# Two written instruction orders, VectorE's and ScalarE's, changed in a fused conformer and SSD block

## The chip, the cores and the metric

The kernel runs on one core of a Trainium2 chip. The metric is the device time of one execution in microseconds, and the figure compared is the median of several runs. One more execution was recorded by the hardware profiler; all durations below are from it. The engines are called as in the profile: PE is TensorE, which multiplies matrices (PEld is its loading of weights), DVE is VectorE, ACT is ScalarE, POOL is GpSimd, and SP is SyncE, which only issues loads and stores here.

## The reference: what is computed

One block of a network on 512 tokens of width 1024, in float32. Cut to what matters:

```python
h = rms_norm(x, mix_pre_g)
proj = h @ w_in                       # u_glu, z, x/B/C, dt and two gates
v = val * sigmoid(gt)                 # of u_glu + glu_b
v = silu(layer_norm(causal_depthwise_conv(v, 31 taps)))
conv_out = v @ pw_w + pw_b
x, B, C = silu(causal_depthwise_conv(xbc, 4 taps))
y = ssd_chunked(x, dt, a, B, C, d_skip) * silu(z)
y = y * rsqrt(mean(y * y over each of 8 groups) + eps) * norm_g
ssm_out = y @ out_w
mixed = (g_conv * conv_out + g_ssm * ssm_out) @ w_out
x = x + rms_norm(mixed)
x = x + rms_norm((silu(g) * u) @ w_down)   # g, u of rms_norm(x) @ w_gate_up
```

`ssd_chunked` is the state-space scan: inside a chunk of tokens it forms C B^T, weighs it with a lower triangle of decays exp(a_cs[l] - a_cs[s]) and multiplies it with x dt; between chunks it carries a state.

## The kernel before

**Products.** Every factor is held as a high part, rounded to the format fp32r, and a low part, the remainder; `mm3` (L423) makes each product of three matmuls, high by high (L425), low by high (L427 or L431, by the side) and high by low. Activations are split once. Weights are split as they arrive: SP loads 512 KB into one of five `raw` buffers (L382), ScalarE casts the high part `whi` (L390), and VectorE subtracts it from raw to make `wlo` (L397). For every second block of the scan ScalarE writes the negated high part (L394) and a GpSimd DMA adds the raw weights to it (L395). `whi` and `wlo` have five buffers each, in rotation; in the w_out stage some blocks use a second pair, `chi` and `clo`. A `raw` buffer is loaded again once both of its readers are done.

**Stages.** (1) Norm and the gated projection, to about 103 us. (2) The scan, to about 510 us, in 8 groups g. For a group, `proj_x` and `proj_bc` project x (two tiles), B and C into PSUM; `conv4` runs the 4-tap convolution on each, a scaled copy by ScalarE (L887, the step x_g_e.0), three taps by VectorE (L889) and a SiLU by ScalarE (L893). `make_L` (from L670) broadcasts the running sums into the tile L by a GpSimd DMA, masks it by a GpSimd `affine_select` (L675), and ScalarE takes 16 exponentials of it (L681). `s1` (L943) transposes x on TensorE into `pxT`, in two halves, each in its own bank, from which VectorE makes `xdt` (L957), part of `y` (L958) and `xdec` (L962); it also forms C B^T (`pcb`) and multiplies L by it (L973). `s2` (L976) forms the chunk states (`pSa`, `pSb`, from `xdec`), the carried states `prev` (L985, L988) and the diagonal part `yd`. `s3` (L999) adds the part from the carried state (`yo`, L1013), multiplies by silu(z), and normalises: squares on ScalarE (`jk`, L1032), the mean and the power on GpSimd (`power`, `pm` at L436, `rs` at L437), and a scaled copy on ScalarE (`y`, L1035). `s4` (L1039) transposes y (`pyT`) and splits it into a high part by ScalarE (L1050) and a low part by VectorE (L1051); both are called `yhl`. `proj_zz` (L922) projects z for two groups at once, four tiles `pz`, each emptied by ScalarE in two SiLUs, `zb` (L938) and `z` (L939). `ssm_out` multiplies finished pairs of groups by the output weights (`pso`). Between these stand the taps of the 31-tap convolution, on VectorE (`tap`, L698; a0 to a7 are the eight tiles of channels), with the first tap of each on ScalarE (L695), and sums over channels (`vsum`, L1155). (3) The gates and the rest of `ssm_out`, to about 600 us. (4) The pointwise product of the convolution branch, in forms that save products (from L1258), about 600 to 641 us; it ends in `mixed` (L1269), which adds the two branches in `pd` (L1270) and splits them into `m0h`, `m1h` (ScalarE, L1273) and `m0l`, `m1l` (VectorE, L1274), for the two halves of the tokens. (5) w_out (`tm_wo`, about 631 to 686 us), whose result is normalised and added to the input rows `xr` (L1468), loaded through ScalarE's queue, as is the gain `gpost0` (L1385). (6) The feed-forward part, to the end.

**Banks.** PSUM has eight banks. The scan's short-lived tiles (`pxT`, `pyT`, `pSa`, `pYa`) take three of them in turn, the projections (`px`, `pB`, `pC`, `pz`, `pso`) another three in turn, and `yd`, `pBT` and `pcb` the other two. A tile that TensorE wants to write waits until the tile that stood in its bank has been read: the second half of a pxT waits for `yhl` of the pyT that is three places before it, the fourth `pz` for `zb` and `z` of the first.

**Orders.** Nothing decides at run time. Five lists of names, one per engine, give the order in which each executes: `ORDER_ACT` (from L94), `ORDER_DVE` (from L164), `ORDER_PE` (from L250), `ORDER_POOL` (L260) and `ORDER_SP` (L273). `in_written_order` (L338) counts each engine's instructions by the tile they write, calls them name.0, name.1 and so on, and ties each to the one before it in the list, without a semaphore; an engine takes its instructions one after the other, and one that waits holds up all behind it. A DMA that ScalarE issues stands in its list like any other step. In ScalarE's list y1.0 is the scaled copy of L1035, in VectorE's list y1.4 is one of the products of `s3`; x0_1.1 is in ScalarE's list the SiLU of the second x tile of group 0, in VectorE's its second tap.

Of the kernel before, what the change touches and what calls it, by code (L numbers as in the profile page):

```python
# [61 lines left out]
for _n, _c in PRM:  # L62
# [36 lines left out]
    "h_t13.3 h_t42.0 h_t42.2 h_t42.1 h_t13.1 sg2.0 h_t42.3 sg3.0 z0.2 whi_11S.0 whi_11s.0 z0.0 whi_11C.0 z0.3 a0.0 "  # L99
    "z0.1 whi_13S.0 v4.0 v5.0 v4.1 whi_15A.0 a1.0 sg4.0 scratch.0 whi_13C.0 whi_17A.0 wlo_17A.0 v6.0 v5.1 sg5.0 "  # L100
    "whi_15S.0 whi_13s.0 sg4.2 whi_15C.0 whi_17S.0 sg4.1 sg5.2 whi_19.0 sg5.1 v7.0 v6.1 wlo_19.0 sg6.0 sg6.1 "
    "whi_17C.0 whi_20.0 v7.1 sg7.0 sg6.2 whi_21.0 wlo_21.0 whi_22.0 cd.0 scratch.2 eacs.0 sg7.2 whi_23.0 scratch.3 "
    "wlo_23.0 scr.3 sg7.1 whi_24.0 scr.0 x0_0.0 scr.1 dec.0 whi_25.0 scr.2 wlo_25.0 x0_1.0 x0_0.1 whi_26.0 B0.0 "
    "x0_1.1 L0.0 L0.4 L0.2 L0.1 L0.5 L0.3 C0.0 L0.7 L0.8 L0.6 L0.9 B0.1 C0.1 L0.10 x1_0.0 L0.14 x1_1.0 L0.11 L0.12 "
    "L0.13 L0.15 whi_27.0 x1_0.1 BT0.0 wlo_27.0 whi_28.0 whi_29.0 L1.0 B1.0 prev0.0 wlo_29.0 whi_30.0 L1.1 x1_1.1 "
    "B1.1 L1.2 C1.0 whi_31.0 L1.3 wlo_31.0 L1.4 L1.5 L1.6 L1.7 L1.8 L1.9 z1.0 C1.1 jk.0 L1.10 jk.1 whi_32.0 z1.1 jk.2 "
    "jk.3 L1.15 L1.11 L1.13 L1.14 x2_0.0 y0.1 L1.12 y0.2 y0.0 L2.0 y0.3 whi_33.0 whi_34.0 wlo_33.0 whi_35.0 BT1.0 "
    "x2_1.0 wlo_35.0 x2_0.1 L2.2 B2.0 L2.1 yhl0.0 whi_36.0 L2.4 prev1.0 B2.1 x2_1.1 L2.3 L2.5 C2.0 whi_37.0 L2.6 "
    "wlo_37.0 yhl0.1 C2.1 L2.7 L2.8 L2.9 L2.10 jk.4 L2.11 jk.5 L2.12 jk.6 L2.13 jk.7 L2.14 L2.15 L3.0 L3.1 L3.2 L3.3 "
    "y1.0 y1.1 zb2_0.0 z2.0 zb2_0.1 z2.1 y1.2 y1.3 L3.4 zb2_1.0 whi_38.0 z2.2 whi_39.0 whi_40.0 wlo_39.0 zb2_1.1 z2.3 "  # L110
# [6 lines left out]
    "zb4_0.0 z4.0 zb4_0.1 z4.1 y3.0 y3.1 y3.2 y3.3 zb4_1.0 z4.2 L5.14 whi_54.0 whi_55.0 whi_56.0 wlo_55.0 zb4_1.1 "  # L117
    "whi_57.0 x5_0.0 whi_58.0 a4.0 z4.3 a5.0 yhl2.2 yhl2.3 x5_1.0 L5.15 BT4.0 whi_59.0 wlo_57.0 B5.0 x5_0.1 whi_60.0 "
    "wlo_59.0 whi_61.0 x5_1.1 prev4.0 wlo_61.0 B5.1 whi_62.0 C5.0 whi_63.0 wlo_63.0 C5.1 L6.0 whi_64.0 L6.1 L6.2 L6.3 "
# [63 lines left out]
    "prev1.1 a1.29 vsum.0 C2.0 C2.1 C2.2 yhl0.1 yo1.0 yo1.1 y1.4 y1.5 wlo_38.0 wlo_40.0 x3_0.0 x3_0.1 wlo_42.0 x3_0.2 "  # L183
# [1789 lines left out]
```

## Time and profile before

| | us |
|---|---|
| median of 3 runs | 1014.97 (1014.56 to 1015.54) |
| the profiled execution | 1014.45 |
| its span | 1012.7 |
| PE busy | 1001.7 (99%) |
| PEld busy | 881.7 (87%) |
| DVE busy | 875.5 (86%) |
| ACT busy | 672.7 (66%) |
| POOL busy | 124.0 (12%) |

The span goes from the first to the last recorded instruction; 1.75 us of the profiled execution lie around it. Shares are of the span. TensorE was granted 0.999 of its full clock. A row of a timeline gives the start, the duration, the engine, the line, the operation with its output and inputs, and in brackets the idle time of the engine before it and what released it. In the list of waits a row gives who waited for whom, the sum, the number of times and the longest. In the chain of waits a row gives a start, a duration and what stood on the chain. In the table by stage a row gives the stretch and its length, and then for PE, PEld, DVE, ACT and POOL the busy time and the number of instructions, the granted clock, the share of the DMA engines and GB/s. Durations in a timeline overlap a little, because the next instruction starts before the last has drained: the distance from start to start is what one costs. A row of a helper such as `mm3` carries the helper's line, so the tile's name tells the stage.

### The profile page before, as it was taken

How to read it: one execution, taken by the hardware profiler on the slowest of the kernel's cores; microseconds unless marked ns; L12 is line 12 of the kernel's file. 1: busy time of each engine (PE TensorE's matmuls, PEld its weight loads, DVE VectorE, ACT ScalarE, POOL GpSimd, SP SyncE). 2: the span in 40 equal slices, each digit the busy share in tenths (PEclk: the TensorE clock that was granted, in tenths of full speed). 3: DMA queues.
4: the chain of work that ended last, by engine and by line, in shares of the span. 5: the costliest groups of instructions: out<-in, count | busy, mean ns of one | idle time of the engine just before them, and what ended most of it. 6: DMA issues, size and time to landing. Idle time of an engine off the chain costs nothing.

```text
span 1012.7 us, 16327 instructions
## 1 busy us (share of the span) xinstructions
PE 1001.7 (99%) x6296; PEld 881.7 (87%) x6296; DVE 875.5 (86%) x1285; ACT 672.7 (66%) x1104; POOL 124.0 (12%) x145
## 2 busy tenths in 40 slices
PE   9999999999999999999999999999999999999997
PEld 7899889878888888888888889889999999998886
DVE  7898999828997999899996688779999897899974
ACT  8577798898667756873442585587666566668552
POOL 0210211110123122110110020011000000001001
PEclk9999999999999999999999999999999999999999
DMA  8756945637641874365452256636555455469622
GB/s 299 215 133 154 256 121 148 186 95 177 167 146 23 212 188 121 97 157 141 104 134 94 83 116 210 216 109 165 184 146 167 147 146 146 135 178 290 210 84 83
DMA packets 44557, 156.62 MB, mean 155 GB/s; under 512 B 5184, under 2 KB 6208, under 8 KB 43456
## 3 DMA queue, kind: packets, MB, share of 16 engines
q1 hardware_dynamic: 30672, 105.44, 30.9%
q0 software_dynamic: 11888, 44.57, 22.5%
q10 hardware_dynamic: 1920, 5.57, 1.6%
q8 instruction: 49, 0.80, 0.3%
q14 instruction: 28, 0.23, 0.1%
HBM read 151.31 MB, written 4.26 MB: 154 GB/s over the span
## 4 chain that ended last, share of the span: by engine, by line
PE 80%; ACT 9%; DVE 7%; POOL 1%; issue 1%; DMA 1%; POOLq 0%; DVEq 0%; ACTq 0%; SPq 0%
PE xy L431 4%; PE xy L425 4%; PE xy L427 4%; PE pso L425 3%; PE pso L431 3%; PE pso L427 3%; PE yv L431 2%; PE yv L427 2%; PE yv L425 2%; DVE a L698 2%; PE px L425 2%; PE px L427 2%; PE px L431 2%; ACT whi L390 2%; PE pgs L431 1%; PE pgc L425 1%
## 5 line engine op out<-in xcount | busy, mean ns | idle before, releaser
L698 DVE SCALAR_TENSOR_TENSOR a<-v,prm_t,a 128x507 f32<-128x507 f32 (+19 forms) x240 | 171.9, 760 | 0.5
L390 ACT CAST whi<-raw 128x1024 fp32r<-128x1024 f32 x91 | 94.4, 1046 | 87.6 <-PE pso L427 42.5
L397 DVE TENSOR_TENSOR wlo<-raw,whi 128x1024 fp32r<-128x1024 f32 x54 | 65.7, 1220 | 34.3 <-ACT whi L390 34.3
L395 POOL DMA_DIRECT2D wlo<-in_w x37 | 32.9, 890 | 283.3 <-ACT wlo L394 97.8
L425 PE MATMUL pz<-whi,hhi 128*128 128x512 f32 (+2 forms) x160 | 55.6, 353 | 1.1 <-ACT z L939 1.1
L431 PE MATMUL pz<-whi,hlo 128*128 128x512 f32 (+2 forms) x160 | 56.1, 352 | 0.0
L427 PE MATMUL pz<-wlo,hhi 128*128 128x512 f32 (+2 forms) x160 | 55.8, 350 | 0.0
L1406 ACT CAST whi_g<-raw 128x1024 fp32r<-128x1024 f32 x40 | 41.4, 1052 | 14.7 <-DVE raw L1437 8.4
L425 PE MATMUL pso<-yhl,whi 128*128 128x512 f32 x128 | 50.8, 399 | 0.0
L431 PE MATMUL pso<-yhl,wlo 128*128 128x512 f32 x128 | 50.4, 395 | 0.0
L425 PE MATMUL px<-hhi,whi 128*128 128x512 f32 x128 | 50.4, 394 | 0.0
L427 PE MATMUL pso<-yhl,whi 128*128 128x512 f32 x128 | 50.3, 395 | 0.0
L427 PE MATMUL px<-hlo,whi 128*128 128x512 f32 x128 | 49.9, 390 | 0.0
L431 PE MATMUL px<-hhi,wlo 128*128 128x512 f32 x128 | 49.9, 389 | 0.0
L681 ACT ACTIVATE L<-L,nacs 128x128 f32<-128x128 f32 x128 | 42.9, 392 | 4.1 <-POOL L L675 3.9
L1411 DVE TENSOR_TENSOR wlo_g<-raw,whi_g 128x1024 fp32r<-128x1024 f32 x34 | 41.2, 1220 | 4.0 <-ACT whi_g L1406 4.0
L889 DVE SCALAR_TENSOR_TENSOR x<-px,prm_t,x 128x511 f32<-128x511 f32 (+2 forms) x48 | 35.7, 744 | 6.9 <-ACT x L887 6.7
L394 ACT ACTIVATE wlo<-whi 128x1024 fp32r<-128x1024 f32 x37 | 39.2, 1059 | 0.2
L425 PEld LDWEIGHTS pz<-whi,hhi 128*128 128x128 f32 x160 | 30.1, 188 | 5.3 <-ACT z L939 1.5
L431 PEld LDWEIGHTS pz<-whi,hlo 128*128 128x128 f32 x160 | 30.2, 189 | 3.8
L427 PEld LDWEIGHTS pz<-wlo,hhi 128*128 128x128 f32 x160 | 30.2, 188 | 3.8
L1406 ACT CAST chi_g<-raw 128x1024 fp32r<-128x1024 f32 x24 | 24.9, 1053 | 10.4 <-DVE raw L1437 3.6
(1046 smaller groups left out, 3625.1 us busy)
## 6 DMA issues: line engine op xcount, KB each, us to landing
raw<-in_w SPq DMA_DIRECT2D x182, 512.0 KB, 4.4
wlo<-in_w POOLq DMA_DIRECT2D x37, 512.0 KB, 5.9
L<-scr POOLq DMA_DIRECT2D x8, 1024.0 KB, 5.2
wlo_g<-in_w POOLq DMA_DIRECT2D x11, 512.0 KB, 5.9
sums<-in_w POOLq DMA_DIRECT2D x16, 256.0 KB, 4.9
clo_g<-in_w POOLq DMA_DIRECT2D x6, 512.0 KB, 5.6
pw_raws<-in_w SPq DMA_DIRECT2D x4, 512.0 KB, 8.0
xr<-in_x ACTq DMA_DIRECT2D x4, 512.0 KB, 5.0
```

The lines of the kernel that those rows point to most:

```text
L390: act.copy(hi[:, c], src)
L394: act.activation(lo[:, c], hi[:, c].bitcast(F32), AF.Copy, scale=-1.0)
L395: pool.dma_start(lo[:, c], w[n][:, c].bitcast(F32R), accum_op=ALU.add)
L397: dve.tensor_tensor(out=lo[:, c], in0=src, in1=hi[:, c].bitcast(F32), op=ALU.subtract)
L425: pe.matmul(ps, lh, rh, start=start, stop=False, skip_group_check=more)
L427: pe.matmul(ps, lh, rl, start=False, stop=False, skip_group_check=more)
L431: pe.matmul(ps, ll, rh, start=False, stop=stop, skip_group_check=more)
L681: act.activation(L[:, h, c, :], L[:, h, c, :], AF.Exp, bias=nacs[:, c, HG * g + h : HG * g + h + 1])
L698: return dve.scalar_tensor_tensor(out=va[j][:, d:], in0=vs[j][:, : T - d], scalar=col("dw_w", j * KC + KC - 1 - d), in1=va[j][:, d:], op0= ...
L889: dve.scalar_tensor_tensor(out=a[:, d:], in0=ps[:, : T - d], scalar=col("ssm_w", i * KS + KS - 1 - d), in1=a[:, d:], op0=ALU.mult, op1=ALU ...
L1406: act.copy(hi, src)
L1411: dve.tensor_tensor(out=lo, in0=src, in1=hi.bitcast(F32), op=ALU.subtract)
```

## The change

`ORDER_ACT` and `ORDER_DVE` are written anew; the other three lists stay. Both hold the same names as before (1006 and 1285), each once, so no instruction is added, removed or altered. The names that stand elsewhere lie in eight stretches of the lists, named here by their times in the profile of before:

1. 58 to 78 us: casts and subtractions of weight blocks 11 and 13, and copies in the gated projection.
2. 110 to 160 us, groups 0 and 1: ScalarE's x0_1.1, B0.1 and C0.1 among the exponentials L0; whi_27 and wlo_27 earlier; VectorE's steps on B0 and C0 side by side, xdt0.1 ahead of xdt0.0.
3. 200 to 222 us: ScalarE's yhl0.1 and y1.0 to y1.3 move behind zb2_0.0 and z2.0, L3.4 ahead of them; VectorE's yhl0.1 behind wlo_40, yo1.1 ahead of yo1.0.
4. 326 to 350 us: VectorE's yhl2.2 ahead of a4.1, vsum.2 and wlo_58, behind xdt4.0; ScalarE's a4.0 and x5_0.0 earlier, a5.0 and whi_58 later.
5. 427 to 455 us: VectorE's yhl4.2 ahead of a5.29, x7_0.2, vsum.4, a7.0 and a6.1; xdec6.0 behind x7_1.2, B7.0, a6.1 and so.8; ScalarE's wlo_73, whi_75, L7.15 and wlo_75 later, yhl4.2, yhl4.3 and B7.0 earlier.
6. 508 to 523 us: small moves of y7, sgs and yhl6.
7. 604 to 637 us: the hand-over from the pointwise product, `pd` and the casts of blocks 99 to 105.
8. 636 to 665 us: VectorE's wlo_111 and pd3_1.1, pd3_1.2 ahead of clo_110; ScalarE's m1h.3 ahead of whi_111, and its loads xr0 and xr1 behind whi_111, gpost0 behind m1h.5.

The core of the diff (every line is one of a list's lines; "..." where lines are left out):

```diff
--- before.py
+++ after.py
@@ ORDER_ACT @@
-    "x0_1.1 L0.0 L0.4 L0.2 L0.1 L0.5 L0.3 C0.0 L0.7 L0.8 L0.6 L0.9 B0.1 C0.1 L0.10 x1_0.0 L0.14 x1_1.0 L0.11 L0.12 "
...
-    "wlo_37.0 yhl0.1 C2.1 L2.7 L2.8 L2.9 L2.10 jk.4 L2.11 jk.5 L2.12 jk.6 L2.13 jk.7 L2.14 L2.15 L3.0 L3.1 L3.2 L3.3 "
-    "y1.0 y1.1 zb2_0.0 z2.0 zb2_0.1 z2.1 y1.2 y1.3 L3.4 zb2_1.0 whi_38.0 z2.2 whi_39.0 whi_40.0 wlo_39.0 zb2_1.1 z2.3 "
...
-    "zb4_0.0 z4.0 zb4_0.1 z4.1 y3.0 y3.1 y3.2 y3.3 zb4_1.0 z4.2 L5.14 whi_54.0 whi_55.0 whi_56.0 wlo_55.0 zb4_1.1 "
-    "whi_57.0 x5_0.0 whi_58.0 a4.0 z4.3 a5.0 yhl2.2 yhl2.3 x5_1.0 L5.15 BT4.0 whi_59.0 wlo_57.0 B5.0 x5_0.1 whi_60.0 "
...
-    "wlo_71.0 a6.0 whi_74.0 zb6_1.1 y5.3 y5.2 z6.3 x7_0.0 wlo_73.0 y5.0 a7.0 L7.15 whi_75.0 yhl4.2 x7_1.0 yhl4.3 "
...
-    "yhl6.1 prev7.0 sgs1.0 wlo_83.0 whi_84.0 sgs2.0 whi_85.0 jk.28 sgs3.0 jk.29 wlo_85.0 jk.30 jk.31 whi_86.0 y7.0 "
-    "y7.1 y7.2 y7.3 sgs4.0 whi_87.0 yhl6.2 yhl6.3 sgs5.0 wlo_87.0 whi_88.0 whi_89.0 whi_90.0 whi_91.0 whi_92.0 sgs6.0 "
...
-    "whi_106.0 m1h.2 m0h.2 whi_107.0 m1h.5 m0h.5 m0h.4 m1h.1 m1h.4 chi_108.0 xr0.0 xr1.0 whi_111.0 chi_109.0 m0h.3 "
-    "gpost0.0 whi_112.0 m1h.3 chi_110.0 m0h.6 m1h.6 m0h.7 m1h.7 jk0_a0.0 jk1_a0.0 jk0_b0.0 x2d.0 jk1_b0.0 jk0_a1.0 "
...
+    "whi_27.0 L0.2 L0.8 L0.1 wlo_27.0 L0.7 L0.3 x1_0.0 L0.0 C0.1 x0_1.1 B0.1 L0.9 whi_28.0 L0.11 L0.13 L0.6 L0.5 "
...
+    "C2.1 L2.13 L2.9 L2.7 L2.12 L2.11 L2.14 L2.10 L3.0 L3.3 jk.4 L3.2 L3.4 L2.15 jk.5 L3.1 jk.6 L2.8 jk.7 zb2_0.0 "
+    "z2.0 zb2_0.1 yhl0.1 whi_38.0 z2.1 y1.1 y1.0 whi_39.0 whi_40.0 y1.3 zb2_1.0 y1.2 z2.2 wlo_39.0 zb2_1.1 z2.3 "
...
+    "zb4_0.0 z4.0 zb4_0.1 z4.1 y3.0 y3.1 y3.2 y3.3 zb4_1.0 z4.2 L5.14 whi_54.0 whi_55.0 wlo_55.0 whi_56.0 a4.0 x5_0.0 "
+    "whi_57.0 zb4_1.1 z4.3 yhl2.2 yhl2.3 x5_1.0 whi_58.0 wlo_57.0 whi_59.0 L5.15 BT4.0 B5.0 a5.0 whi_60.0 prev4.0 "
...
+    "wlo_71.0 zb6_1.1 whi_74.0 x7_0.0 z6.3 y5.2 a6.0 y5.0 y5.3 yhl4.2 yhl4.3 BT6.0 x7_1.0 wlo_73.0 B7.0 a7.0 x7_0.1 "
...
+    "yhl6.1 prev7.0 sgs1.0 wlo_83.0 whi_84.0 sgs2.0 whi_85.0 sgs3.0 jk.28 jk.29 wlo_85.0 jk.30 jk.31 whi_86.0 y7.3 "
+    "y7.0 y7.2 y7.1 sgs4.0 sgs5.0 yhl6.2 yhl6.3 whi_87.0 wlo_87.0 whi_88.0 whi_89.0 whi_90.0 whi_91.0 whi_92.0 sgs6.0 "
...
+    "pd3_1.0 m0h.2 whi_107.0 m0h.3 m0h.5 m1h.2 m0h.4 chi_108.0 chi_109.0 m1h.4 m1h.1 m1h.3 whi_111.0 xr0.0 xr1.0 "
+    "m1h.5 gpost0.0 whi_112.0 chi_110.0 m0h.6 m0h.7 m1h.7 jk0_a0.0 m1h.6 jk1_a0.0 jk0_b0.0 jk1_b0.0 x2d.0 jk0_a1.0 "
...
@@ ORDER_DVE @@
-    "v3.0 h_t42.3 wlo_11S.0 scratch.2 wlo_11s.0 wlo_11C.0 raw13.1 v3.1 v1.1 v4.0 v2.1 scratch.1 scratch.3 scratch.0 "
...
-    "wlo_24.0 a1.9 a0.9 x0_1.0 a0.10 x0_1.1 a1.10 x0_1.2 a0.11 a1.11 wlo_26.0 B0.0 a0.12 B0.1 a1.12 B0.2 a0.13 C0.0 "
-    "a1.13 C0.1 a0.14 C0.2 a1.14 a0.15 a1.15 a0.16 a1.16 x1_0.0 xdt0.0 a0.17 x1_0.1 a1.17 x1_0.2 xdt0.1 xdec0.0 L0.0 "
...
-    "prev1.1 a1.29 vsum.0 C2.0 C2.1 C2.2 yhl0.1 yo1.0 yo1.1 y1.4 y1.5 wlo_38.0 wlo_40.0 x3_0.0 x3_0.1 wlo_42.0 x3_0.2 "
...
-    "x5_0.0 x5_0.1 a4.0 x5_0.2 a4.1 yhl2.2 xdt4.0 x5_1.0 x5_1.1 wlo_58.0 yhl2.3 L4.0 xdt4.1 x5_1.2 xdec4.0 B5.0 y4.1 "
...
-    "a6.1 yhl4.2 x7_1.0 yhl4.3 x7_1.1 xdt6.0 x7_1.2 xdt6.1 L6.0 xdec6.0 y6.0 B7.0 y6.1 B7.1 so.8 B7.2 so.9 wlo_76.0 "
...
-    "a7.25 yhl6.2 yhl6.3 a6.26 a7.26 so.16 a6.27 a7.27 so.17 a6.28 wlo_88.0 so.18 a7.28 a6.29 so.24 so.19 a7.29 "
...
-    "pd3_0.2 clo_108.0 m0l.2 clo_109.0 m0l.3 m0l.4 m0l.5 pd3_0.3 clo_110.0 wlo_111.0 pd3_1.1 pd3_1.2 wlo_112.0 m0l.6 "
...
+    "raw13.1 scratch.2 v3.0 wlo_11S.0 scratch.0 v1.1 wlo_11s.0 h_t42.3 scratch.3 v4.0 scratch.1 wlo_11C.0 wlo_13S.0 "
...
+    "wlo_24.0 a1.9 a0.9 x0_1.0 a0.10 x0_1.1 x0_1.2 a0.11 a1.10 a1.11 a0.12 a1.12 B0.0 a0.13 wlo_26.0 B0.1 B0.2 C0.0 "
+    "C0.1 a1.13 a0.14 a0.15 C0.2 a1.14 a1.15 a1.16 x1_0.0 a0.16 x1_0.1 a1.17 xdt0.1 xdt0.0 y0.1 xdec0.0 y0.0 x1_1.0 "
...
+    "prev1.1 a1.29 vsum.0 C2.0 C2.1 C2.2 yo1.1 yo1.0 y1.4 y1.5 wlo_38.0 wlo_40.0 yhl0.1 x3_0.0 x3_0.1 wlo_42.0 x3_0.2 "
...
+    "wlo_56.0 x5_0.1 x5_0.2 xdt4.0 yhl2.2 x5_1.0 x5_1.1 L4.0 y4.0 yhl2.3 x5_1.2 xdt4.1 xdec4.0 B5.0 a4.1 B5.1 "
...
+    "a5.25 a4.26 a4.27 a5.26 a4.28 wlo_72.0 a4.29 a5.27 wlo_74.0 a5.28 a6.0 x7_0.0 vsum.3 x7_0.1 yhl4.2 a5.29 x7_0.2 "
+    "x7_1.0 yhl4.3 xdt6.0 xdt6.1 x7_1.1 L6.0 y6.0 x7_1.2 B7.0 a6.1 so.8 xdec6.0 B7.1 a7.0 B7.2 vsum.4 so.9 y6.1 "
...
+    "yhl6.2 yhl6.3 a6.26 a7.24 a7.25 a6.27 a7.26 so.16 a7.27 so.17 a6.28 wlo_88.0 so.18 a7.28 a6.29 so.24 so.19 a7.29 "
...
+    "wlo_107.0 m0l.3 pd3_0.2 m0l.5 clo_108.0 pd3_0.3 clo_109.0 m1l.2 m1l.1 m0l.4 wlo_111.0 pd3_1.1 pd3_1.2 clo_110.0 "
...
```

117 rows, old and new, of tables (ORDER_ACT, ORDER_DVE) are left out of this document.

## The prediction

> **What bounds the kernel now.** I read the page first, then the list of waits for TensorE, then TensorE's own timeline around each wait, and last the chain of waits and the other engines' timelines backwards from each of them.
>
> ```profile
> PE 1001.7 (99%) x6296; PEld 881.7 (87%) x6296; DVE 875.5 (86%) x1285; ACT 672.7 (66%) x1104; POOL 124.0 (12%) x145
> ```
>
> TensorE is busy for 1001.7 of 1012.7 us and its work is the same in both kernels: the change can win only what TensorE waits, and can lose whatever new waits it makes. The waits, in the view that groups them:
>
> ```profile
> PE tm_wo L431 <- DVE m0l L1274: 1.1, 1, 1.1
> PE pz L425 <- ACT z L939: 1.1, 1, 1.1
> PE warm_ps L509 <- DVE woken L504: 1.0, 1, 1.0
> PE pxT L954 <- DVE yhl L1051: 0.8, 2, 0.5
> PE ptr L1503 <- ACT mg L1490: 0.5, 1, 0.5
> ```
>
> Five rows, six waits, 4.5 us in all. The warm_ps wait is start-up. The ptr wait I call **E**; the written orders around it are not changed, and I leave it as it is. Four remain, A to D; their true price is the distance between starts, less the 0.23 that lies between two matmuls of 128x512 that wait for nothing (the first two rows of A).
>
> **A, B, C, D, each from TensorE's timeline.** First A:
>
> ```profile
> 211.74 0.39 PE L427 MATMUL pz<-wlo,hhi 128*128 128x512 f32 x1
> 211.96 0.39 PE L431 MATMUL pz<-whi,hlo 128*128 128x512 f32 x1
> 213.45 0.50 PE L425 MATMUL pz<-whi,hhi 128*128 128x512 f32 x1 [1.10 <-ACT z L939]
> ```
>
> A costs 213.45 - 211.96 - 0.23 = 1.26. Then B and C, the same place two and four groups later:
>
> ```profile
> 336.87 0.39 PE L427 MATMUL pB<-hlo,whi 128*128 128x512 f32 x1
> 337.53 0.65 PE L954 MATMUL pxT<-ident,x 128*128 128x128 f32 x4 [0.27 <-DVE yhl L1051]
> ```
>
> ```profile
> 442.17 0.39 PE L431 MATMUL pB<-hhi,wlo 128*128 128x512 f32 x1
> 443.09 0.66 PE L954 MATMUL pxT<-ident,x 128*128 128x128 f32 x4 [0.53 <-DVE yhl L1051]
> ```
>
> B costs 0.66 - 0.23 = 0.43, C 0.92 - 0.23 = 0.69. D, in the w_out stage:
>
> ```profile
> 653.35 0.39 PE L427 MATMUL tm_wo<-wlo,m0h 128*128 128x512 f32 x1
> 654.88 0.50 PE L431 MATMUL tm_wo<-whi,m0l 128*128 128x512 f32 x1 [1.15 <-DVE m0l L1274]
> ```
>
> D costs 1.53 - 0.23 = 1.30. A to D are 3.68 us, 0.36% of the time; that is the ceiling of the gain.
>
> **The change part by part.** It adds and removes no instruction; it permutes two engines' lists. DMA issues that stand in ScalarE's list (xr0, xr1, gpost0) move too; the queues of SP and GpSimd keep their orders.
>
> *Place 3, about 200 to 222 us (wait A).* TensorE needs z2.0 out of its bank. ScalarE's rows:
>
> ```profile
> 208.79 1.85 ACT L681 ACTIVATE L<-L,nacs 128x128 f32<-128x128 f32 x6
> 210.54 0.89 ACT L1035 ACTIVATE y<-y,rs 128x256 f32<-128x256 f32 x2
> 211.44 1.28 ACT L938 ACT_TABLE_LOAD   x1
> 212.74 0.38 ACT L938 ACTIVATE zb<-pz 128x256 f32<-128x256 f32 x1
> 213.02 0.38 ACT L939 ACTIVATE z<-pz 128x256 f32<-128x256 f32 x1
> ```
>
> ```profile
> 231.43 0.68 ACT L1050 ACTIVATE yhl<-pyT,prm_t 128x512 fp32r<-128x512 f32 x1
> ```
>
> The new list takes y1.0 and y1.1 (0.89) and yhl0.1 (0.6, as its sister at 231.43) from ahead of z2.0 and puts L3.4 (1.85 / 6 = 0.3) ahead of it: z2.0 ends near 213.40 - 1.2 = 212.2, when TensorE asks (211.96 + 0.23 = 212.19). A goes, with nothing to spare: **1.26 gained**. But the work is not gone. y1.0 to y1.3 now stand between z2.1 and z2.2, mixed with whi_38 to whi_40; whi_39 waits for the weight slot that TensorE gives back at the end of the z tile, so the two table loads saved here don't carry past it, and behind it ScalarE is by 222 us where it was. Its yhl0.2 then comes at the old time while TensorE comes 1.26 earlier. VectorE's copy ends 1.47 after ScalarE's start, at 232.90:
>
> ```profile
> 232.15 0.75 DVE L1051 SCALAR_TENSOR_TENSOR yhl<-pyT,prm_t,yhl 128x512 fp32r<-128x512 f32 x1 [1.78 <-ACT yhl L1050]
> ```
>
> ```profile
> 233.62 0.60 PE L954 MATMUL pxT<-ident,x 128*128 128x128 f32 x4
> ```
>
> pxT2's second half started at 233.62, so its margin was 0.72; brought forward by 1.26 it waits about 0.55 to 0.65. So A nets about **0.65**; the bounds are 0 (all of it paid back there, if ScalarE is later than I think) and 1.26 (if it is 0.6 earlier at yhl0.2).
>
> *Place 4, about 326 to 350 us (wait B).* VectorE's row that ends it:
>
> ```profile
> 336.72 0.75 DVE L1051 SCALAR_TENSOR_TENSOR yhl<-pyT,prm_t,yhl 128x512 fp32r<-128x512 f32 x1
> ```
>
> yhl2.2 goes ahead of a4.1 and vsum.2 (0.66 each by the pair of rows at place 5), and x5_0.0, which held it up in VectorE's list, no longer stands behind whi_57 and zb4_1.1 in ScalarE's. Against that xdt4.0 (0.60) comes ahead of it, and this needs the first four transposes of pxT4:
>
> ```profile
> 334.28 0.60 PE L954 MATMUL pxT<-ident,x 128*128 128x128 f32 x4
> ```
>
> 334.88 + 0.60 + 0.75 puts the end of yhl2.2 at 336.2, 0.9 before TensorE asks (336.87 + 0.23). **0.43 gained**, bounds 0 and 0.43. Late next would be wlo_58, put behind five steps of about 0.7; nobody asks for it before pB5's next weights, over 1.5 us later.
>
> *Place 5, about 427 to 455 us (wait C).* The five steps a5.29, x7_0.2, vsum.4, a7.0 and a6.1 no longer stand ahead of yhl4.2. One wlo does, as before. At 0.66 each (441.62 to 442.28 below) yhl4.2 ends some 3.3 us before its old end of 443.03 and TensorE's demand at 442.40 is met: **0.69 gained**. But here the cover is thin:
>
> ```profile
> 441.62 0.75 DVE L698 SCALAR_TENSOR_TENSOR a<-v,prm_t,a 128x510 f32<-128x510 f32 x1
> 442.28 0.75 DVE L1051 SCALAR_TENSOR_TENSOR yhl<-pyT,prm_t,yhl 128x512 fp32r<-128x512 f32 x1
> ```
>
> ```profile
> 441.00:461.00 20.00, 19.47 (x142) 15.74 (x141) 20.00 (x30) 10.38 (x15) 1.73 (x2) 1.00 0.64 157
> ```
>
> In that row of the table by stage VectorE (the third busy figure, behind PE and PEld) is busy 20.00 of 20.00: a5.29, a7.0 and vsum.4 are only pushed behind x7_1, L6 and B7.0, and xdec6.0 too moves behind B7.0, a6.1 and so.8. Step by step from yhl4.2, with pxT6's second half at 442.4, I bring x7_1.2 to its end at 448.4; B7.0, a6.1 (0.66 each), so.8 (0.60) and xdec6.0 (0.96) follow, to 451.3.
>
> ```profile
> 452.61 1.02 PE L984 MATMUL pSa<-xdec,BT 128*128 128x256 f32 x4
> ```
>
> TensorE, 0.69 earlier, asks for xdec6.0 at 451.92: a margin of 0.6. If that is not there, C is paid back at pSa6. Bounds 0 and 0.69.
>
> *Places 7 and 8, about 604 to 665 us (wait D).* The chain of waits before D:
>
> ```profile
> 642.16 5.69 DMA raw<-in_w
> 647.87 1.05 ACT whi L390
> 649.23 0.96 ACT chi L390
> 650.21 1.23 DVE clo L397
> 651.43 1.14 DVE wlo L397
> 652.57 0.79 DVE pd L1277 x2
> 653.36 1.13 DVE wlo L397
> ```
>
> Behind chi_110 VectorE ran clo_110, wlo_111, two pd steps and wlo_112, then m0l.6. The new list puts wlo_111 (1.14) and the two pd steps (0.79) ahead of clo_110, into the time in which VectorE waited for chi_110 anyway. Only clo_110, wlo_112 and m0l.6 are left: 1.2 + 1.1 + 0.4 behind 650.21 = 652.9, against TensorE's demand at 653.58. **1.30 gained**, even if raw112 lands no sooner. It may land sooner, because the three 512 KB loads xr0, xr1 and gpost0 are now issued later, and m1h.3 is out of ScalarE's way. The bounds are 0.9 (raw112 1.0 later than now, if whi_107's slot comes late) and 1.30.
>
> *Places 1, 2 and 6 (58 to 78, 110 to 160 and 508 to 523 us).* TensorE has no wait in any of them, so nothing is to be gained; the cost is what the moves make late. In 1 and 6 the moved casts keep over 1 us. In 2 one margin is thin: x0_1.1, which stood ahead of all of L0's exponentials, goes behind six of them, a cast, x1_0.0 and C0.1. By adding these I get its end at 136.5, and TensorE asks at 136.9. I take -0.1 there, between 0 and the price of the second rival, and -0.1 for other small waits.
>
> **Sum**: 0.65 + 0.43 + 0.69 + 1.30 - 0.2 = 2.9 us. Against the profiled execution, 1014.45 (span 1012.7), that gives 1011.55; the median of the runs, 1014.97, stands 0.52 above it, so I predict **1012.1** for the median.
>
> **Rivals.** *First, what is gained is paid back.* A wholly at yhl0.2, C wholly in the stretch where VectorE is full; B and D stay: 0.43 + 1.30 - 0.2 = 1.5, or 1013.5. For it speaks the row of 441 to 461, against it the sums above, which leave 0.6 of A and the whole of C.
>
> *Second, slower: place 2 hangs on GpSimd.* GpSimd's mask of L0 must end before any exponential:
>
> ```profile
> 126.85 1.87 ACT L681 ACTIVATE L<-L,nacs 128x128 f32<-128x128 f32 x6 [2.87 <-POOL L L675]
> ```
>
> ```profile
> 312.27 8.57 POOL pm L436
> ```
>
> ```profile
> L394 ACT ACTIVATE wlo<-whi 128x1024 fp32r<-128x1024 f32 x37 | 39.2, 1059 | 0.2
> ```
>
> ```profile
> 136.78 1.03 PE L954 MATMUL pxT<-ident,x 128*128 128x128 f32 x8
> ```
>
> The pm row is a step on 4 columns that lasted 8.57 us while VectorE ran tap after tap, and ended when VectorE went idle. If the mask is held up in the same way, x0_1.1 comes late, since it now needs six exponentials (1.85), wlo_27 (1.06), x1_0.0, a table load (1.28) and two more steps behind the mask, 6 us in all; from 126.85 that is 132.9, so the first 4 us of delay are free, and 8.57 stalls TensorE 4.6. The change then ends at 1012.1 + 4.6 = 1016.7. It decides from a mask delay of 4 us, and the whole is slower than before from 6.9. Against it: in the new list four steps that read PSUM (B0.1, B0.2, C0.0, C0.1) run there in a row, unlike the taps beside pm, and in the old one the mask got in.
>
> The Trainium skill's page "SBUF — State Buffer", section "Who interferes with whom", says that VectorE steps with two SBUF inputs and GpSimd share a port pair as an exclusive lock, which whoever issues first holds for one whole instruction. By that rule a mask would wait for one tap at most, some 0.7, and this rival would cost nothing (1012.1); the pm row, over a dozen taps long, speaks for a longer hold, so I keep it with a small chance.
>
> *Third, the orders change nothing that TensorE sees*: each wait is ended by a slower partner that I have not seen (A by the table load moved with it, D by raw112's load): 1014.9.
>
> **How the numbers follow.** Chances: forecast (1011.3 to 1012.9) 0.55; no payback at all, 3.7 gained and 1011.3 or below, 0.08; first rival 0.22; second 0.09; third 0.06. A measurement tells about 0.2% from no change, 2.0 us, so faster means under 1012.9: the forecast but for a tenth of it, and the case without payback, 0.57. Slower, over 1017.0, needs the second rival at its worst or a loss unseen, 0.08. The rest, 0.35, is within. The range goes from 1010.9 (all four waits, and the lowest of the runs 0.4 under the median) to 1015.6, over the first and third rivals and part of the second; the forecast's own is 1011.3 to 1012.9.
>
> **What would show it.** In TensorE's waits the rows of pz and tm_wo gone, the pxT row with one new entry at group 2 (near 232.5) of about 0.6 and none at groups 4 and 6; TensorE's start of the first pB7 matmul about 1.8 us earlier, of the last tm_wo about 3. A pxT0 wait for x at 136.9 would speak for the second rival; a wait of pSa6 for xdec near 452 for the first. I am wrong if the pz wait stands, or if new waits of more than 1 us appear.

## The result, and the profile after

The changed kernel takes **1010.45 us** (median of 4 runs, 1009.73 to 1011.18). The kernel before, run beside it, took 1015.25 (4 runs, 1014.56 to 1016.99). The ratio is 0.995, with a 95% interval of 0.9933 to 0.9967: faster by 3.4 to 6.8 us. The forecast was 1012.1, so the gain is larger than reckoned, and the time lies 0.45 under the lower end of the range.

The profiled execution took 1011.07, 3.38 less than that of before; its span is 1009.3. The busy row of its page first, then all of its waits for TensorE:

```profile
PE 1000.1 (99%) x6296; PEld 881.9 (87%) x6296; DVE 876.5 (87%) x1285; ACT 670.9 (66%) x1102; POOL 123.9 (12%) x145
```

```profile
PE ptr L1503 <- ACT mg L1490: 1.7, 2, 1.5
PE warm_ps L509 <- DVE woken L504: 1.0, 1, 1.0
```

The rows of tm_wo, pz and pxT are gone. ScalarE has two instructions fewer (1102 for 1104): two loads of its function table, which the order of place 3 no longer needs. But the row of ptr has grown from 0.5 to 1.7, with one wait of 1.5 in it.

TensorE's timeline of the changed kernel, at A, at the place where A was to be paid back, at B, at C, at pSa6, and at D (start, duration, then the instruction; an idle time would stand in brackets):

```profile
211.59 0.39 PE L431 MATMUL pz<-whi,hlo 128*128 128x512 f32 x1
211.82 0.39 PE L425 MATMUL pz<-whi,hhi 128*128 128x512 f32 x1
...
231.60 0.40 PE L427 MATMUL pB<-hlo,whi 128*128 128x512 f32 x1
231.84 0.60 PE L954 MATMUL pxT<-ident,x 128*128 128x128 f32 x4
...
335.04 0.40 PE L427 MATMUL pB<-hlo,whi 128*128 128x512 f32 x1
335.27 0.60 PE L954 MATMUL pxT<-ident,x 128*128 128x128 f32 x4
...
439.80 0.39 PE L431 MATMUL pB<-hhi,wlo 128*128 128x512 f32 x1
440.02 0.60 PE L954 MATMUL pxT<-ident,x 128*128 128x128 f32 x4
...
449.26 0.39 PE L431 MATMUL pso<-yhl,wlo 128*128 128x512 f32 x1
449.49 1.02 PE L984 MATMUL pSa<-xdec,BT 128*128 128x256 f32 x4
...
650.14 0.39 PE L427 MATMUL tm_wo<-wlo,m0h 128*128 128x512 f32 x1
650.37 0.39 PE L431 MATMUL tm_wo<-whi,m0l 128*128 128x512 f32 x1
```

At each of them the starts are 0.22 to 0.24 apart: TensorE waits at none. The new wait is one tile of tokens later than the old E, at ptr3, the transposes of the last tile (E is ptr2). TensorE there in the changed kernel, and at the same place before:

```profile
691.14 0.28 PE L431 MATMUL xy<-b21h,wlo_g 128*128 128x256 f32 x1
692.93 1.27 PE L1503 MATMUL ptr<-ident,mg 128*128 128x128 f32 x8 [1.52 <-ACT mg L1490]
```

```profile
696.33 0.28 PE L431 MATMUL xy<-b21h,wlo_g 128*128 128x256 f32 x1
696.45 1.15 PE L1503 MATMUL ptr<-ident,mg 128*128 128x128 f32 x8
```

To see where the time went I set the start of every matmul against the start of the same one before. The distance grows in steps: 1.26 at A, and 0.11 more at a matmul behind it; 0.42 at B; 0.69 at C; 0.11 near 620; 1.31 at D, and 0.11 at each of three matmuls behind it. Together these are **4.23 us**. At E, near 680, it grows by 0.29, which I don't credit to the change, since it does so in p3, p126, p45 and d_rest too, where the order there is that of before (in d_swap and starve it does not). At 692.93 it shrinks again by **1.68** (in the old order that start lay 0.11 behind the one ahead of it, here 1.79). A shift of 0.33 ahead of 11 us and 0.2 in smaller steps fill the rest, to 3.36 earlier at the end.

**Why ptr3 waits.** ScalarE's step ahead of it, GpSimd's step ahead of that, and VectorE's timeline of the same 4 us, of the changed kernel:

```profile
692.16 1.33 ACT L1490 ACTIVATE mg<-xr,rs_b 128x512 f32<-128x512 f32 x2 [2.76 <-POOL rs_b L1350]
```

```profile
689.46 2.67 POOL L1350 TENSOR_TENSOR rs_b<-pm_b,neg_half 128x1 f32<-128x1 f32 x1 [3.27 <-DVE pm_b L1347]
```

```profile
689.23 0.68 DVE L1436 TENSOR_TENSOR raw<-s,raw 128x512 f32<-128x512 f32 x1
689.83 0.69 DVE L1434 TENSOR_TENSOR s<-raw 128x512 f32<-128x512 f32 x1
690.43 0.69 DVE L1520 TENSOR_TENSOR t3l<-t,t3h 128x512 fp32r<-128x512 f32 x1
691.03 0.69 DVE L1520 TENSOR_TENSOR t4l<-t,t4h 128x512 fp32r<-128x512 f32 x1
693.63 0.69 DVE L1507 TENSOR_TENSOR xg<-ptr,prm_t 128x512 f32<-128x512 f32 x1 [1.90 <-PE ptr L1503]
```

rs_b, a power on one column, lasts 2.67 us, while VectorE starts an instruction every 0.60; it ends 0.4 after VectorE has run dry. The same two places before:

```profile
694.66 0.86 POOL L1350 TENSOR_TENSOR rs_b<-pm_b,neg_half 128x1 f32<-128x1 f32 x1 [3.27 <-DVE pm_b L1347]
```

```profile
695.70 0.69 DVE L1434 TENSOR_TENSOR s<-raw 128x512 f32<-128x512 f32 x1 [0.59 <-DMA raw<-in_w]
```

There VectorE stood still for 0.59, waiting for a load (raw115), and rs_b was done in 0.86. The written orders of this stretch are the same in both kernels. What differs is when raw115 lands: by the trace's records of the transfers it took 4.27 us from issue to landing in this execution, against 5.11 before, and was there before VectorE asked.

### The profile page after: what moved, and what is told of

Its sections match the earlier page's. It is cut to its first block, busy times and chain, and to the rows that moved or that the text cites. A ratio compares the mean times of both kernels' runs of the same rounds, so it can differ in the third digit from the quotient of the medians.

```text
span 1009.3 us, 16312 instructions
## 1 busy us (share of the span) xinstructions
PE 1000.1 (99%) x6296; PEld 881.9 (87%) x6296; DVE 876.5 (87%) x1285; ACT 670.9 (66%) x1102; POOL 123.9 (12%) x145
## 4 chain that ended last, share of the span: by engine, by line
PE 97%; DVE 1%; ACT 1%; DMA 1%; POOL 0%; issue 0%; SPq 0%; POOLq 0%; DVEq 0%; ACTq 0%
PE xy L425 4%; PE xy L427 4%; PE xy L431 4%; PE pso L425 3%; PE pz L427 3%; PE pz L431 3%; PE pz L425 3%; PE pso L431 3%; PE pso L427 3%; PE px L425 3%; PE px L427 3%; PE px L431 3%; PE yv L427 2%; PE yv L425 2%; PE yv L431 2%; PE yd L996 2%
## 5 line engine op out<-in xcount | busy, mean ns | idle before, releaser
L698 DVE SCALAR_TENSOR_TENSOR a<-v,prm_t,a 128x507 f32<-128x507 f32 (+20 forms) x240 | 172.5, 762 | 0.7
```

Of the source, the lines that this page charges most:

```text
L698: return dve.scalar_tensor_tensor(out=va[j][:, d:], in0=vs[j][:, : T - d], scalar=col("dw_w", j * KC + KC - 1 - d), in1=va[j][:, d:], op0= ...
```

## The experiments

Every kernel ran beside the kernel before, whose medians were 1014.86 (p3, d_swap, fix, after_again), 1015.15 (starve, fix2, p45, p126) and 1015.22 (after3, fix2b, d_rest, nop2). In p3, d_swap and fix every line number is 4 higher than in the other kernels.

### after_again: the changed kernel once more

It has no edit.

> The changed kernel a second time. Its profile had a new wait of TensorE at the transposes of the third token tile (ptr, 1.5 us at 692.9): GpSimd's rs_b took 2.67 us there instead of 0.86, while VectorE ran back to back. Theory S (GpSimd is held off while VectorE has no idle moment; VectorE has none there whenever the raw block it needs next has landed in time): the wait is there in the slower runs and missing in the faster, so the time is either near 1011.1 with a wait of 1.4 to 1.7 in the profile, or near 1009.8 without it. Rival: the wait is always there and the two groups of times (1011.1 and 1009.8) differ in something else, such as the start.

Measured: 1009.47 (8 runs, 1008.22 to 1011.52), ratio 0.9951 (0.9938 to 0.9965). Its profiled execution took 1009.22 and has no wait at ptr3; GpSimd and VectorE there:

```profile
689.64 0.86 POOL L1350 TENSOR_TENSOR rs_b<-pm_b,neg_half 128x1 f32<-128x1 f32 x1 [3.27 <-DVE pm_b L1347]
```

```profile
689.42 0.68 DVE L1436 TENSOR_TENSOR raw<-s,raw 128x512 f32<-128x512 f32 x1
690.11 0.69 DVE L1434 TENSOR_TENSOR s<-raw 128x512 f32<-128x512 f32 x1
```

What follows: with the same lists rs_b took 0.86 once and 2.67 once. Here raw115 took 4.53 us, 0.26 longer, and VectorE's two starts lie 0.69 apart instead of 0.60. So the wait is not fixed by the order; it hangs on a break of under 0.1 us in VectorE's work.

### p3: place 3 alone, on the kernel before

```
 ORDER_ACT
- L3.3 y1.0 y1.1 zb2_0.0 z2.0 zb2_0.1 z2.1 y1.2 y1.3 L3.4 ...
+ jk.7 zb2_0.0 z2.0 zb2_0.1 yhl0.1 whi_38.0 z2.1 y1.1 y1.0 whi_39.0 ...
 ORDER_DVE
- C2.2 yhl0.1 yo1.0 yo1.1 ...
+ C2.2 yo1.1 yo1.0 y1.4 y1.5 wlo_38.0 wlo_40.0 yhl0.1 ...
```

> Place 3 alone. The prediction: wait A gone (1.26) but 0.55 to 0.65 paid back at pxT2, net -0.65. Rival, from the trace of the changed kernel, where nothing was paid back: -1.4 and no pxT2 wait, since ScalarE is 2.5 us earlier from wlo_39 on and not where it was. Waits B, C, D and E unchanged in size.

Measured: 1014.24 (10 runs), ratio 0.9993 (0.9981 to 1.0006), not told from no change by the time. The trace is clear, though: the step at A is 1.26 + 0.11, and pxT2 gives nothing back:

```profile
231.58 0.40 PE L431 MATMUL pB<-hlo,whi 128*128 128x512 f32 x1
231.82 0.60 PE L958 MATMUL pxT<-ident,x 128*128 128x128 f32 x4
```

What follows: place 3 alone wins the whole of A in TensorE's trace; the prediction's payment back doesn't happen. The profiled execution took 1013.04; near 700, where the lists are those of before, it lost 0.83 at two matmuls of the feed-forward part, because raw115 came late and VectorE waited 1.41 us for it.

### p45 and p126: the other places of the scan, on the kernel before

```
 p45, ORDER_DVE (places 4 and 5; ORDER_ACT's lines of both places too)
- a4.1 yhl2.2 xdt4.0 ...
+ xdt4.0 yhl2.2 ... B5.0 a4.1 ...
- a6.1 yhl4.2 x7_1.0 ... L6.0 xdec6.0 y6.0 B7.0 ...
+ yhl4.2 a5.29 x7_0.2 x7_1.0 ... B7.0 a6.1 so.8 xdec6.0 ...
 p126, ORDER_ACT (places 1, 2 and 6; ORDER_DVE's lines of all three too)
- B0.0 x0_1.1 L0.0 L0.4 ...
+ B0.0 C0.0 whi_27.0 L0.2 L0.8 L0.1 wlo_27.0 L0.7 L0.3 x1_0.0 L0.0 C0.1 x0_1.1 ...
```

> Places 4 and 5 alone. The prediction: waits B (0.43) and C (0.69) gone, -1.1, if xdec6.0 keeps its 0.6 of margin; A, D and E stay. Its first rival: C is paid back at pSa6, near 452, and the gain is 0.4.

> Places 1, 2 and 6 alone. The prediction: no TensorE wait made or removed, within 0.2 us. Its second rival: GpSimd's mask of L0 is held off and TensorE waits for x0_1.1 at pxT0, up to 4.6 us. Theory S says that VectorE's list has breaks there (pairs of steps of which the second reads what the first wrote), so that the mask gets in, but is stretched.

Measured: p45 1013.43 (10 runs), ratio 0.9978 (0.9961 to 0.9994); B's step is 0.42 and C's 0.69, and neither is paid back, at pSa6 or elsewhere. p126 1014.05 (10 runs), ratio 0.9992 (0.9979 to 1.0005); no wait at pxT0. The waits of p45, places that its lists don't touch:

```profile
PE ptr L1503 <- ACT mg L1490: 1.7, 2, 1.5
PE pz L425 <- ACT z L939: 1.7, 1, 1.7
```

What follows: B and C are won as reckoned, and places 1, 2 and 6 cost nothing at the places that they touch. And two things not looked for. The 1.5 us wait at ptr also occurs in the old order there (rs_b lasted 2.67 in this execution), so it is not a product of the change. And the old waits differ in size from one execution to the next: that at pz was 1.7 here, 1.1 before and 0.4 in p126. p45's profiled execution (1016.01) was the slowest of its ten; by starts TensorE also lost 0.74 near 146, at pSb0, and p126's lost 1.4 more than before in the stretch of D, again where their lists are those of before.

### d_swap and d_rest: which part of places 7 and 8 ends D

```
 d_swap, ORDER_DVE, on the kernel before
- clo_110.0 wlo_111.0 pd3_1.1 pd3_1.2 wlo_112.0 m0l.6
+ wlo_111.0 pd3_1.1 pd3_1.2 clo_110.0 wlo_112.0 m0l.6
 d_rest: all other moves of places 7 and 8 in both lists, without these
```

> Of places 7 and 8 only one thing: VectorE's wlo_111, pd3_1.1 and pd3_1.2 ahead of clo_110. The prediction: this alone ends wait D, even with raw112 landing no sooner (m0l.6 ends near 652.9 against a demand at 653.58): -1.3 to -1.6. Rival: the gain at D came from raw112 landing 3.2 us sooner, and the swap alone gains under 0.5.

> Places 7 and 8 alone, without the one swap of d_swap. The prediction says the swap is what ends wait D; without it the earlier issue of raw112 is left. In the changed kernel raw112 landed 6.4 us sooner by the clock, 3.2 of it against the work around it, more than the 1.1 that m0l.6 was too late by. So this should end D too (-1.3 to -1.7), and the two cures are each enough. Rival: raw112 lands sooner only together with the other places' moves, and D stays above 0.8.

Measured: d_swap 1013.84 (10 runs), ratio 0.9989 (0.9974 to 1.0004); D's steps are 1.31 + 3 times 0.11, the whole of D. raw112 was issued at 641.97 and landed at 647.50, against 642.16 and 647.85 before: the issue is sooner by 0.19, as much as TensorE is here, and the landing by 0.35. VectorE in d_swap, at wlo_112 and m0l.6:

```profile
651.19 1.22 DVE L401 TENSOR_TENSOR wlo<-raw,whi 128x1024 fp32r<-128x1024 f32 x1
652.33 0.42 DVE L1278 TENSOR_TENSOR m0l<-pd,m0h 128x256 fp32r<-128x256 f32 x1
```

m0l.6 ends at 652.75, as the prediction had it (652.9), and TensorE takes it at 653.38 without a wait. d_rest: 1012.15 (10 runs), ratio 0.9971 (0.9959 to 0.9984), and D is gone there too, by the same steps. (In d_swap's execution B is missing as well, a step of 0.42, though nothing was moved there: an old wait can be absent by chance.) raw112 was issued at 641.17 there and landed at 644.65, 3.2 sooner than before. ScalarE's whi_112, which waited for it until 647.87 before, starts at 645.86 without a wait. clo_110 is still the first, but it runs at 647.88, and m0l.6 ends at 652.51:

```profile
647.88 1.23 DVE L397 TENSOR_TENSOR clo<-raw,chi 128x1024 fp32r<-128x1024 f32 x1 [1.05 <-ACT chi L390]
...
652.09 0.42 DVE L1274 TENSOR_TENSOR m0l<-pd,m0h 128x256 fp32r<-128x256 f32 x1
```

What follows: either half of the edit ends D by itself. The swap does it as the prediction reckoned; the rest does it by the earlier load that the prediction left as a "may".

### starve and fix2: is it the break in VectorE's work that decides?

starve takes the kernel before and puts s1_2.0, the step that waits for raw115, behind t3l and t4l, so that VectorE has no reason to stop. fix2 takes the changed kernel and puts there a step that needs the result of the one ahead of it (raw114.1), which makes a short break, and moves s1_2.0 out of the stretch.

```
 starve, ORDER_DVE, on the kernel before
- pm_b3.0 raw114.0 s1_2.0 t3l.0 t4l.0 xg3_0.0
+ pm_b3.0 raw114.0 t3l.0 t4l.0 s1_2.0 xg3_0.0
 fix2, ORDER_DVE, on the changed kernel
- raw114.0 s1_2.0 t3l.0 t4l.0 xg3_0.0 t1_3.0 t2_3.0 t1l.1 ... raw114.1
+ raw114.0 raw114.1 t3l.0 t4l.0 xg3_0.0 t1_3.0 t2_3.0 t1l.1 s1_2.0 ...
```

> The kernel before, and in VectorE's list s1_2.0 (which in its profile waited 0.59 us for raw115 just after pm_b3) moved behind t4l.0, so that VectorE runs raw114, t3l, t4l, s1_2 with no break. Theory S (GpSimd's rs_b cannot end until VectorE has a break): rs_b takes about 2.6 us in place of 0.86, mg3 and ptr3 come late, a new ptr wait of 1.4 to 1.7, and the kernel is that much slower. Rival (rs_b's length in the changed kernel had another cause, such as DMA traffic): rs_b stays at 0.86, no new wait, time unchanged.

> The changed kernel, and in VectorE's list raw114.1, which reads what raw114.0 writes, put right behind it, and s1_2.0 in its place further back, behind t1l.1. VectorE then has a break of some 0.03 us between the two, whenever raw115 lands, and loses no time. Theory S: rs_b 0.86, no ptr wait and no wait for t1h or t1l, so the time is that of the changed kernel in its faster profile, about 5.2 us under before, each time. Rival (a break as short as that does not let GpSimd in): rs_b 2.2 us or longer and the ptr wait of 1.4 to 1.7 in the profile.

Measured: starve 1016.04 (10 runs), ratio 1.0007 (0.9994 to 1.0021). GpSimd, VectorE and TensorE of its profile:

```profile
693.45 2.66 POOL L1350 TENSOR_TENSOR rs_b<-pm_b,neg_half 128x1 f32<-128x1 f32 x1 [3.27 <-DVE pm_b L1347]
```

```profile
693.23 0.68 DVE L1436 TENSOR_TENSOR raw<-s,raw 128x512 f32<-128x512 f32 x1
...
695.03 0.68 DVE L1434 TENSOR_TENSOR s<-raw 128x512 f32<-128x512 f32 x1
```

```profile
696.92 1.27 PE L1503 MATMUL ptr<-ident,mg 128*128 128x128 f32 x8 [1.52 <-ACT mg L1490]
```

rs_b's 2.66 and the wait of 1.52 are those of the changed kernel to 0.01, made by a move of one step. In the median 0.9 us show; the interval holds no change, and the kernel before has this wait in a part of its executions already, as p45 shows for its order. fix2 measured 1010.04 (4 runs, 1009.84 to 1010.22), ratio 0.9948 (0.9933 to 0.9963):

```profile
689.60 0.86 POOL L1350 TENSOR_TENSOR rs_b<-pm_b,neg_half 128x1 f32<-128x1 f32 x1 [3.27 <-DVE pm_b L1347]
```

```profile
689.38 0.68 DVE L1436 TENSOR_TENSOR raw<-s,raw 128x512 f32<-128x512 f32 x1
690.09 0.69 DVE L1437 TENSOR_TENSOR raw<-raw 128x512 f32<-128x512 f32 x1
```

What follows: two starts 0.71 apart instead of 0.60 are enough for rs_b to get in (0.86), and the wait at ptr is gone. So it is the unbroken run of VectorE that holds rs_b off. All fourteen profiles divide the same way: where the start of raw114.0 and the next lie 0.60 apart, rs_b takes 2.66 or 2.67 (the changed kernel, starve, p45); where they lie 0.65 (nop2) or more apart, it takes 0.85 or 0.86 (the other eleven). fix2 costs 0.22 us of its own near 706, where a step that was moved comes late.

### fix: the same wait, another cure

```
 ORDER_DVE, on the changed kernel
- pm_b3.0 raw114.0 s1_2.0 t3l.0 t4l.0 xg3_0.0
+ pm_b3.0 raw114.0 xg3_0.0 s1_2.0 t3l.0 t4l.0
```

> The changed kernel, and in VectorE's list xg3_0.0 (which waits for the transposes ptr3) moved up from behind t4l.0 to right behind raw114.0, so that VectorE goes idle just after pm_b3. Theory S: GpSimd's rs_b ends some 0.5 us after that idle moment begins (near 690.3), the ptr wait of 1.4 to 1.7 goes, and the time is 1009.7 or less, with no slower group of runs. Rival (rs_b is long for a reason of its own, or waits for pm_b): rs_b stays near 2.7 us, the wait stays, and the time does not move or gets worse by the delay of t3l and t4l.

Measured: 1010.82 (8 runs, 1010.36 to 1011.13), ratio 0.9958 (0.9945 to 0.9972). rs_b took 0.86, because VectorE now waits for ptr there, and the ptr wait is gone. But s1_2, t3l and t4l run after that and hold up t1l: TensorE waits for t1h and t1l, 0.71 and 0.55 by starts. The wait has moved, and nothing is won.

### after3 and fix2b: the changed kernel and fix2 side by side

They have no edit beyond those of the changed kernel and of fix2.

> The changed kernel once more, beside fix2b on one chip. Its runs should spread as before (some 3 us from lowest to highest), because whether rs_b is held off hangs on the landing of raw115; the profile shows either rs_b near 2.67 us with a ptr wait of 1.5, or 0.86 without.

> fix2 again, beside the changed kernel on one chip. Theory S: no ptr wait, rs_b 0.86; the median is between 0 and 1.5 us under that of after3 (0.7 if half of after3's runs have the wait), and the highest run is lower than after3's highest by 1 us or more. Rival: fix2 differs from the changed kernel only by its two moved steps' own delay (0.2 us at 706), and is not faster.

Measured: after3 1009.98 (6 runs, 1008.89 to 1011.48), ratio 0.9949 (0.9934 to 0.9965); fix2b 1010.13 (6 runs, 1009.43 to 1010.54), ratio 0.9949 (0.9935 to 0.9963). The profile of after3 has a third form of the same stretch. VectorE, and two of its waits:

```profile
692.28 0.69 DVE L1434 TENSOR_TENSOR s<-raw 128x512 f32<-128x512 f32 x1 [1.95 <-DMA raw<-in_w]
```

```profile
PE v L425 <- ACT t1h L1519: 0.7, 1, 0.7
PE v L427 <- DVE t1l L1520: 0.4, 1, 0.4
```

raw115 took 6.47 us here; VectorE stood still for 1.95 ahead of s1_2.0, rs_b took 0.86, and what is late is t1l. What follows: one transfer, in 4.27, 4.53 or 6.47 us, puts a wait at ptr (1.68), none, or two later ones (0.82 and 0.56 by starts). fix2 narrows the spread (1.1 us against 2.6) but its median is not lower, contrary to what was hoped for; no version tried beats the changed kernel.

### nop2: the change without place 2

```
 ORDER_ACT and ORDER_DVE: the lines of place 2 as before, all else changed
+ B0.0 x0_1.1 L0.0 L0.4 L0.2 L0.1 L0.5 L0.3 C0.0 ...
- B0.0 C0.0 whi_27.0 L0.2 L0.8 L0.1 wlo_27.0 L0.7 L0.3 x1_0.0 L0.0 C0.1 x0_1.1 ...
```

> The changed kernel without place 2. The prediction gave place 2 nothing (-0.1). Rival, from the profile of p45, where TensorE waited 0.74 us for VectorE's y at pSb0 (146.4) with the old order of place 2, and from the runs of kernels with that order, which spread over 4 to 5 us: place 2's old order makes TensorE wait in some executions, so this kernel's median is 0.3 to 1.0 above the changed kernel's and its runs spread more.

Measured: 1009.87 (6 runs, 1009.21 to 1011.45), ratio 0.9951 (0.9935 to 0.9966), beside 0.9949 for the whole change on the same chip; the 0.3 to 1.0 by which it was to be slower did not come. Place 2 neither gains nor costs what can be measured.

## Why the prediction was right or wrong

**The bound and the direction: right.** TensorE sets the time, its waits were the price, and the four waits went.

**A: the step that failed.** The payment back at pxT2 did not come. The prediction let A net 0.65, because "whi_39 waits for the weight slot that TensorE gives back at the end of the z tile, so the two table loads saved here don't carry past it, and behind it ScalarE is by 222 us where it was". In the list before, whi_39 had waited for nothing; ScalarE ran without a break, and the moment of release only lay near:

```profile
219.24 2.00 ACT L390 CAST whi<-raw 128x1024 fp32r<-128x1024 f32 x2
```

ScalarE in the changed kernel (z2.0, then whi_38, then yhl0.2):

```profile
210.47 0.38 ACT L939 ACTIVATE z<-pz 128x256 f32<-128x256 f32 x1
...
213.38 1.05 ACT L390 CAST whi<-raw 128x1024 fp32r<-128x1024 f32 x1 [1.68 <-PE pz L431]
...
229.06 0.68 ACT L1050 ACTIVATE yhl<-pyT,prm_t 128x512 fp32r<-128x512 f32 x1
```

It does wait for TensorE, but at whi_38, at 213.38, and from there it runs without a break, with one table load where there were three. yhl0.2 starts at 229.06, 2.37 before its old 231.43, and pxT2's second half at 231.84, 1.78 before its old 233.62. The copies keep 0.6 more distance than before, and A is kept: **1.37 instead of 0.65**, the largest miss in the sum. The lesson of the row is in its brackets: without an idle time nobody was waiting there, and a release that lies close in time is no bound. z2.0 ended at 210.85, too, not at 212.2 with "nothing to spare".

**B and C: right**, 0.42 and 0.69 against 0.43 and 0.69. B was absent in d_swap too, with the old order; with the new one both are absent in all eight profiles. The thin cover at pSa6 held; VectorE's row of xdec6.0 in the changed kernel:

```profile
447.50 0.95 DVE L962 TENSOR_TENSOR xdec<-xdt,dec 128x768 f32<-128x768 f32 x1
```

It ends at 448.45, and pSa asks at 449.49: a margin of 1.0, where 0.6 was reckoned. The first rival falls at both its places.

**D: right in mechanism, a term too small.** 1.30 was forecast, 1.31 came at the wait itself, and 0.33 more at the three matmuls behind it. The sum and its ceiling of 3.68 took only the waits; A and D also had followers of 0.11, four in all, and one more stands near 620 by itself. So the second step that failed is the ceiling, "A to D are 3.68 us". The range's lower end, 1010.9, had all of A in it already; what it put at nothing are the 0.55 of these five matmuls, and with them it would lie near 1010.3, just under the 1010.45 measured. Of the sum's miss of 1.36 (4.23 against 2.87), 0.72 is A, 0.34 D's followers, 0.11 the one near 620, and 0.2 the deductions for place 2 and other small waits, which did not come.

One remark under D was wrong in its reason: that xr0, xr1 and gpost0 "are now issued later". ScalarE's compute (ACT) and its DMA issues (ACTq) in the changed kernel:

```profile
638.46 1.05 ACT L390 CAST chi<-raw 128x1024 fp32r<-128x1024 f32 x1 [1.04 <-PE pwx L431]
638.59 0.87 ACTq L1468 DMA_DIRECT2D xr<-in_x  x2
...
639.53 0.42 ACTq L1385 DMA_DIRECT2D gpost<-in_gp  x1
...
641.28 1.05 ACT L390 CAST whi<-raw 128x1024 fp32r<-128x1024 f32 x1
```

In the list chi_109, three m1h and whi_111 stand ahead of xr0; here both xr go out 0.1 us after chi_108 began, and gpost while chi_109 ran, 1.7 ahead of whi_111. By the clock xr goes out 3.1 sooner than before (641.69), about as much as TensorE is ahead here (3.2). What moved against the rest is raw112: SP issued it at 637.85, 0.74 ahead of xr, where before it came 0.47 behind, and it took 3.63 us instead of 5.69. In all eight profiles with the new order of places 7 and 8 it is ahead of xr and takes 3.39 to 3.64; in all six with the old order it is behind and takes 5.19 to 7.14.

**The second rival: its place was wrong, its mechanism real.** At place 2 the mask was held up; GpSimd's row after, and before:

```profile
124.59 3.40 POOL L675 TENSOR_SCALAR_AFFINE_SELECT L<-L 128x2048 f32<-128x2048 f32 x1 [4.58 <-DMA L<-scr]
```

```profile
124.73 2.08 POOL L675 TENSOR_SCALAR_AFFINE_SELECT L<-L 128x2048 f32<-128x2048 f32 x1 [4.26 <-DMA L<-scr]
```

1.3 us of delay lie inside the 4 that were reckoned free, and TensorE waited for nothing there: x0_1.1 ended at 134.70, 1.7 ahead of pxT0 at 136.41. (The prediction gave that step two ends, 136.5 under place 2 and 132.9 here; with the mask 1.3 late the second is near and the first far off.) In after_again, with the same lists, the mask took 2.01, so it is not held each time; what held it was not tested. But a hold of this kind, tested by starve and fix2, struck at ptr3, where the lists were not changed and the prediction had no step: its "other small waits" of 0.1 stood against a wait of 1.68. The criterion "new waits of more than 1 us" was met in this one execution, and not in after_again. The third rival falls with A to D.

The Trainium skill's page "SBUF — State Buffer", section "Who interferes with whom", has GpSimd and VectorE's two-input steps share a port pair that is locked for one whole instruction. The rows here differ in the length: rs_b was ready while the step at 689.23 ran, and by a lock of one instruction would have got in behind it; it stayed out for three more, until VectorE stopped. How the two engines settle it is not visible in a trace; that a break of 0.05 to 0.11 us between two steps suffices is shown by nop2, after_again and fix2.

**What stays open.** The times of the changed kernel lie 4.8 to 5.4 under those of before in the three comparisons, while its steps explain 4.23 less what the stretch near 692 takes (0 to 1.7). The profile of before (1014.45) is a good execution, 0.8 under the median beside the changed kernel, and the old waits at pz and tm_wo were larger in some others. It would fit if the old order waited more on average than in its one profile, but the other profiles with the old order don't bear that out for A: by starts it cost 1.26 before and 1.84, 0.52, 1.11, 0.88 and 0.81 in p45, p126, d_swap, d_rest and starve, 1.07 on average. For D the sizes are 1.31, 1.03, 1.21, 1.67 and 0.81 (before, p3, p45, p126, starve). So 0.6 to 1.2 us of the gain in the medians, and more where ptr3 waits, stay without a cause that the traces show. The parts' gains (1 - ratio: 0.0007, 0.0022, 0.0008 and 0.0029 for p3, p45, p126 and d_rest) add to 0.0066 against 0.005 for the whole, which their intervals allow.

## What to carry to other kernels

Before a stall is said to hold an engine back, look for the idle time in front of that very instruction: without it the engine never waited there, and time saved ahead of it carries on to the next real wait. When transfers and engine lists change, look at small GpSimd steps on the path wherever VectorE may run several instructions without a break, even in stretches whose order is untouched; here a step that depends on the one ahead of it was break enough. Judge a reorder of this size by the traced wait and by several executions, since one load's landing can shift the end by more than one of its parts is worth.

## What was not expected of the hardware

- A GpSimd step on one column lasted 0.85 or 0.86 us with a break in VectorE's work (eleven profiles) and 2.66 or 2.67 without one (three); the shortest break that was enough was 0.05 us (0.65 between starts instead of 0.60, in nop2).
- DMA issues in ScalarE's list went out up to 2.7 us ahead of compute that stands before them in the list (638.59 against 641.28).
- After a wait of TensorE a few of the following matmuls each came 0.11 us later than in the run without the wait: one behind A, three behind D, and the same ones in the other profiles that have these waits.
- A 512 KB load (raw112) took 3.39 to 3.64 us where it was issued ahead of the two xr loads and 5.19 to 7.14 where it was issued behind them.
- One 512 KB load (raw115) took 4.27, 4.53 and 6.47 us in three executions of the same kernel, and each gave another chain of waits.
